# Expert weights streamed one matrix at a time: 1024 columns in 4 KB rows, eight column blocks open in three PSUM banks

## The chip, the cores and the metric

The kernel runs on one core of one Trainium2 chip. The metric is the device time of one execution in microseconds (us); lower is better. All times below come from the runs of the kernel before and from one execution of it under the profiler.

## What is computed

A hybrid encoder block (convolution branch, state-space branch, gated merge) is followed by a mixture of 16 experts. The change lies in the experts alone. Each expert picks the `cap` = 130 tokens of 1040 with the highest affinity, and 16 experts of 1024 x 2048 (gate and up) and 2048 x 1024 (down) run on them, all in float32:

```python
def expert_choice_ffn(xn, w_router, w_gate, w_up, w_down):
    b, T, d = xn.shape
    cap = CAPACITY_FACTOR * T // N_EXPERTS
    aff = jax.nn.softmax(jnp.einsum('btd,de->bte', xn, w_router).astype(jnp.float32), axis=-1)
    top_aff, top_idx = lax.top_k(jnp.swapaxes(aff, 1, 2), cap)
    xg = xn[bi, top_idx]
    hg = jnp.einsum('becd,edf->becf', xg, w_gate)
    hu = jnp.einsum('becd,edf->becf', xg, w_up)
    y = jnp.einsum('becf,efd->becd', jax.nn.silu(hg) * hu, w_down)
    y = y * top_aff[..., None].astype(y.dtype)
    return jnp.zeros_like(xn).at[bi, top_idx].add(y)
```

## The kernel before

The expert stage is a list of 64 steps, four to an expert (`steps`, the loop at the end of the listing), from about 1650 us to the end of the span. A step takes 512 columns of the gate matrix and the same 512 of the up matrix. `load_gu` brings them in four tiles of 1 MB (`wst`, two to a matrix, rows of 2 KB in HBM) into a ring of 11 buffers, which the down matrix shares (`bring`, two tiles to a step, rows of 4 KB); all of these loads go out on SP's queue. The loads run `RUN` = 2 steps ahead.

TensorE multiplies in float16, so a weight tile is split first into a high part `wh` and a rest `wl`. `norms` sums the squares of each tile on ScalarE (into `junk`, L1137); `scales` turns these into one power-of-two scale per matrix (a CAST to `sqb`, two small matmuls into a PSUM tile `rp`, L1109, and five tiny VectorE operations `sc`); `convert` then writes `wh` (half on ScalarE, L1148, half on VectorE, L1149) and `wl` (VectorE, L1151). All of this is done one step ahead. Expert 0's first two steps are native: its raw float32 tiles go into the matmuls.

In `gate_up`, `pair(p)` takes two column blocks of 128 of either matrix: 24 matmuls of 130 columns each fill one block (8 row blocks, times `wh`·x0, `wh`·x1, `wl`·x0), and two blocks share a PSUM tile `gu`, of which there are three. ScalarE then reads the gate tile (`sil`, L1180) and VectorE multiplies in the up tile (`ac`, L1181). A step has two such pairs of 96 matmuls each. From expert 1 on, 16 float32 matmuls of the expert before stand behind each pair (`down`, L1203, PSUM tiles `dn`).

Once per expert three other things pass through. `put` turns the finished outputs of the expert before (four transposes into `rp` for each of four pieces), scales them on VectorE (`yo0`, `yo1`, L1221) and adds them to HBM by indirect DMAs from POOL (L1222); `yo0` comes in step 0 of the next expert, `yo1` at that step's end. `route` (step 1) makes the list of the next expert's tokens (18 small matmuls into `rp`, L1061) and has POOL gather them (`xg`, two indirect DMAs, L1070). `turn` (end of step 2) transposes `xg` on TensorE in four quarters of 8 transposes (L1098), each into an `rp` tile that ScalarE copies to `xT` (L1100). There are two `rp` buffers, and `put`, `route`, `scales` and `turn` share them.

The order on each engine is set when the kernel is built, by a scheduler that keeps each engine's own order fixed at run time; `tc.high_priority` moves an operation forward in it. So an operation that waits holds up all that stands behind it on its engine.

## Time and profile before

| what | value |
|---|---|
| device time, median of 3 runs | 3004.99 us (2998.09 to 3011.6) |
| the profiled execution | 2988.87 us, span 2987.1 us |
| TensorE (PE) busy | 2750.6 us, 92% of the span |
| VectorE (DVE) / ScalarE (ACT) / GpSimd (POOL) busy | 75% / 57% / 21% |
| mean granted TensorE clock | 0.961 of full speed |
| twelve experts, 1828.8 to 2785.4 us | PE 933.46 us busy of 956.60, clock 0.99, DMA share 0.95 |

PE is the matmul engine, PEld its weight loads, SP the engine that issues the weight loads. "busy" counts the time in which at least one instruction of the engine is under way; matmuls overlap in the pipeline, so a matmul's own duration is longer than the distance to the next. A wait is idle time of an engine ended by what is named behind the arrow.

### The profile page before, as it was taken

To read this page: it belongs to the slowest core of one execution; us is meant where nothing else is said; L and a number is where in the kernel's file an instruction comes from. 1 tells how busy PE (TensorE), PEld (TensorE's weight loads), DVE (VectorE), ACT (ScalarE), POOL (GpSimd) and SP (SyncE) were. 2 spreads that over 40 slices of the span, in tenths; PEclk is the share of its full clock that TensorE was granted. 3 is DMA by queue.
4 is the path that set the end of the run, shared out by engine and by line. 5 is a ranking of instruction groups with operands and counts; after the bars stand their busy time and mean duration, and the time that the engine had idled before them with its cause. 6 is when DMAs were issued, how large, how long until landed. Compare 5 with 4: busy or idle time off the path is not lost. (4 is left out here: it accounts for less than half of the span.)

```text
span 2987.1 us, 65478 instructions
## 1 busy us (share of the span) xinstructions
PE 2750.6 (92%) x27584; PEld 2359.5 (79%) x27584; DVE 2240.1 (75%) x3023; ACT 1713.3 (57%) x2549; POOL 616.6 (21%) x688
## 2 busy tenths in 40 slices
PE   6989989989997998989998889999999999999995
PEld 4656656655665666989967889999999999999995
DVE  6867896998896799988456677777767676777663
ACT  6567656565665542444223656766666666666743
POOL 2131132132123113330000002222211112222213
PEclk8999989999998999999999899999999999999997
DMA  5356576565566554424345889999999999999994
GB/s 146 96 160 198 173 214 202 156 197 181 181 180 207 161 176 131 161 61 139 107 141 181 301 291 332 337 327 333 336 322 330 325 332 322 332 338 330 334 323 141
DMA packets 337783, 689.77 MB, mean 231 GB/s; under 512 B 38241, under 2 KB 98049, under 8 KB 337481
## 3 DMA queue, kind: packets, MB, share of 16 engines
q1 hardware_dynamic: 284784, 528.74, 51.4%
q0 software_dynamic: 42624, 125.45, 14.7%
q10 hardware_dynamic: 10080, 31.40, 3.3%
q8 instruction: 216, 3.54, 0.5%
q14 instruction: 79, 0.65, 0.1%
HBM read 610.48 MB, written 75.01 MB: 229 GB/s over the span
## 5 line engine op out<-in xcount | busy, mean ns | idle before, releaser
L97 PE MATMUL gu<-xT,wh 128*128 128x130 f16 x3968 | 698.1, 222 | 2.3 <-ACT sil L1180 2.3
L98 PE MATMUL gu<-xT,wh 128*128 128x130 f16 x3968 | 697.9, 220 | 0.0
L99 PE MATMUL gu<-xT,wl 128*128 128x130 f16 x3968 | 697.1, 220 | 0.8 <-DVE wl L1151 0.8
L1137 ACT ACTIVATE junk<-wst 128x2048 bf16<-128x2048 f32 x248 | 473.7, 1910 | 386.3 <-DMA wst<-in_w_exp_gate_dram 313.1
L1151 DVE SCALAR_TENSOR_TENSOR wl<-wst,sc,wh 128x2048 f16<-128x2048 f32 x248 | 572.7, 2346 | 24.3 <-ACT wh L1148 20.7
L98 PEld LDWEIGHTS <-wh 128*128 128x128 f16 x4856 | 480.4, 99 | 75.5 <-issue 32.6
L97 PEld LDWEIGHTS <-wh 128*128 128x128 f16 x4856 | 474.7, 98 | 52.1 <-issue 9.7
L99 PEld LDWEIGHTS <-wl 128*128 128x128 f16 x4832 | 470.0, 97 | 45.2 <-DVE wl L1151 1.1
L1203 PE MATMUL dn<-ac,wst 128*128 128x130 f32 x3840 | 459.3, 277 | 0.0
L1203 PEld LDWEIGHTS dn<-ac,wst 128*128 128x128 f32 x3840 | 440.7, 191 | 0.0
L1222 POOL DMA_INDIRECT h<-yo,idx x60 | 181.5, 3025 | 910.2 <-DVE yo L1221 758.5
L339 DVE SCALAR_TENSOR_TENSOR co<-ci,ct,co 128x1040 f32<-128x1040 f32 x240 | 323.8, 1349 | 5.5 <-ACT co L336 3.8
L97 PE MATMUL mm<-uh,wh 128*128 128x346 f16 (+3 forms) x888 | 279.4, 315 | 17.4 <-ACT xt L404 8.1
L97 PE MATMUL mm<-uh,wl 128*128 128x346 f16 (+1 forms) x864 | 271.7, 314 | 13.3 <-ACT xt L404 7.0
L98 PE MATMUL mm<-ul,wh 128*128 128x346 f16 (+3 forms) x888 | 279.0, 314 | 0.0
L99 PE MATMUL mm<-uh,wh 128*128 128x346 f16 (+3 forms) x888 | 278.1, 314 | 0.0
L98 PE MATMUL mm<-ul,wl 128*128 128x346 f16 (+1 forms) x864 | 271.2, 314 | 0.0
L99 PE MATMUL mm<-uh,wl 128*128 128x346 f16 (+1 forms) x864 | 271.0, 314 | 0.0
L611 ACT ACTIVATE row<-row,cst 128x128 f32<-128x128 f32 (+1 forms) x576 | 170.8, 378 | 143.4 <-DMA row<-cs_d 123.9
L1148 ACT ACTIVATE wh<-wst,sc 128x2048 f16<-128x2048 f32 x124 | 241.2, 1994 | 16.1 <-DVE sc L1114 15.4
L385 DVE SCALAR_TENSOR_TENSOR po<-pre,sp,po 128x1040 f32<-128x1040 f32 x144 | 185.7, 1296 | 2.4 <-ACT po L382 2.0
L97 PE MATMUL mm<-yh,wh 128*128 128x346 f32 (+1 forms) x480 | 156.9, 333 | 15.6 <-ACT yh L796 8.4
(431 smaller groups left out, 4839.9 us busy)
## 6 DMA issues: line engine op xcount, KB each, us to landing
wst<-in_w_exp_gate_dram SPq DMA_DIRECT2D x128, 1024.0 KB, 7.9
wst<-in_w_exp_up_dram SPq DMA_DIRECT2D x128, 1024.0 KB, 9.7
wst<-in_w_exp_down_dram SPq DMA_DIRECT2D x128, 1024.0 KB, 9.9
wr<-in_w_in_dram POOLq DMA_DIRECT2D x70, 512.0 KB, 6.4
row<-cs_d SPq DMA_DIRECT2D x64, 512.0 KB, 5.0
xk<-xk_d SPq DMA_DIRECT2D x92, 256.0 KB, 3.5
er<-ecs_d SPq DMA_DIRECT2D x120, 128.0 KB, 3.7
xk_d<-xt POOLq DMA_DIRECT2D x40, 256.0 KB, 4.2
```

Of the source, the lines that this page charges most:

```text
L97: pe.matmul(ps, wh(k), xh(k), start=(k == 0), stop=False)
L98: pe.matmul(ps, wh(k), xl(k), start=False, stop=False)
L99: pe.matmul(ps, wl(k), xh(k), start=False, stop=(k == K - 1))
L339: dve.scalar_tensor_tensor(co, ci[:, m:m + T], ct[:, m:m + 1], co, op0=OP.mult, op1=OP.add)
L385: dve.scalar_tensor_tensor(po, pre[:, m:m + T], sp[:, j, m:m + 1], po, op0=OP.mult, op1=OP.add)
L611: act.activation(out=E[:L, j, :L], in_=E[:L, j, :L], func=AF.Relu, scale=-1.0, bias=cs)
L1137: act.activation(out=junk, in_=t[m][b], func=AF.Square, accum_out=sq[:, b, m:m + 1])
L1148: act.activation(out=wh[m][0], in_=t[m][0], func=AF.Copy, scale=sc[:, 1, m:m + 1])
L1151: dve.scalar_tensor_tensor(wl[m][b], t[m][b], sc[:, 1, m:m + 1], wh[m][b], op0=OP.mult, op1=OP.subtract)
L1203: pe.matmul(last["dn"][b // 3][:, b % 3], t[:, k, b * P:b * P + P], ac[:, 2 * i + k], start=(i + k == 0 and b % 3 == 0), stop=(i == 7 and ...
L1222: nc.gpsimd.indirect_dma_start(out=h2_d[b], in_=yo[:, h], in_offset=None, compute_op=OP.add, out_offset=bass.IndirectOffsetOnAxis(ap=r.idx ...
```

## The change

A step still has four tiles of 1 MB, but all from one matrix: 1024 columns of gate in steps 0 and 2, the same columns of up in steps 1 and 3. Each tile holds 256 rows of 4 KB. A step has one scale where it had two. Its eight column blocks are open together, in three PSUM tiles of 3, 3 and 2 blocks, and the loop over rows is outermost: `rows_(b)` runs all 48 matmuls that need tile `b`, so all three `gu` tiles are in use from the first tile to the last, and are read only after it: by ScalarE in a gate step (silu straight into `ac`, the `sil` tile is gone), by VectorE in an up step (into `ac` in place). The matmuls, norms, `wh` and `wl` are as many and as large as before. `turn` becomes a generator: its first quarter comes at the end of step 1, the others at points inside step 2, and its copies to `xT` get a high priority.

```diff
-        junk = sel.tile([P, 4, 512], BF, name="junk")
+        junk = sel.tile([P, 2, D], BF, name="junk")
...
                 for i in range(2):
                     for k0 in (0, 4):
+                        yield
                         ps = mps2.tile([P, 4, 2, HC + 1], F16, name="rp")
...
+                        with tc.high_priority(offset=300):
+                            act.activation(out=self.xT[i][:, k0:k0 + 4].rearrange("p k (h c) -> p k h c", h=2),
+                                           in_=ps[:, :, :, :HC], func=AF.Copy)
...
-            for i in range(2):
-                pe.matmul(ps, onesb, sq[:, i], start=(i == 0), stop=(i == 1))
+            for i in range(4):
+                pe.matmul(ps, onesb, sq[:, i:i + 1], start=(i == 0), stop=(i == 3))
...
-            for w in (w_exp_gate, w_exp_up):
-                for b in range(2):
-                    t = ring.tile([P, 4, 512], F32, name="wst")
...
-                    nc.sync.dma_start(t, w[0, e, 512 * b:512 * b + 512, 512 * q:512 * q + 512].rearrange(
+            for b in range(4):
+                t = ring.tile([P, 2, D], F32, name="wst")
...
+                w = w_exp_up if q % 2 else w_exp_gate
+                nc.sync.dma_start(t, w[0, e, 256 * b:256 * b + 256, q // 2 * D:q // 2 * D + D].rearrange(
...
+            for b in range(4):
+                wh.append(split.tile([P, 2, D], F16, name="wh"))
+                wl.append(split.tile([P, 2, D], F16, name="wl", bufs=6))
+                if b % 2:
+                    dve.tensor_scalar_mul(wh[b], t[b], sc[:, 1:2])
+                else:
+                    act.activation(out=wh[b], in_=t[b], func=AF.Copy, scale=sc[:, 1:2])
+                dve.scalar_tensor_tensor(wl[b], t[b], sc[:, 1:2], wh[b], op0=OP.mult, op1=OP.subtract)
...
+            def rows_(b):
+                if b == 0:
+                    sums.extend(mps2.tile([P, 3, CAP], F32, name="gu", bufs=3) for _ in range(3))
+                for k in (2 * b, 2 * b + 1):
+                    for f in range(KD):
+                        ps, cols = sums[f // 3][:, f % 3], slice(f * P, f * P + P)
+                        opens, ends = k == 0 and f % 3 == 0, k == KD - 1
...
+                        pe.matmul(ps, wh[b][:, k % 2, cols], xT[0][:, k], start=opens, stop=False, skip_group_check=True)
+                        pe.matmul(ps, wh[b][:, k % 2, cols], xT[1][:, k], start=False, stop=False, skip_group_check=True)
+                        pe.matmul(ps, wl[b][:, k % 2, cols], xT[0][:, k], start=False, stop=ends, skip_group_check=True)
+                if b < 3:
+                    return
...
+                        if q % 2:
+                            dve.scalar_tensor_tensor(a_, sums[i][:, :n], s, a_, op0=OP.mult, op1=OP.mult)
                         else:
+                            act.activation(out=a_, in_=sums[i][:, :n], func=AF.Silu, scale=s)
...
-            pair(0)
+            part(0)
+            next(turning, None)
+            part(1)
             next(done, None)
             if prev:
                 down(2 * q, ds[0], prev[0])
+            next(turning, None)
             if raw:
                 ready[coming] = convert(raw, sq)
-            pair(1)
+            part(2)
+            next(turning, None)
+            part(3)
             next(done, None)
             if prev:
                 down(2 * q + 1, ds[1], prev[0])
-            if e + 1 < NE and q == 2:
-                nxt.turn()
+            if e + 1 < NE and q == 1:
+                turning = nxt.turn()
+                next(turning)
+            elif q == 2:
+                for _ in turning:
+                    pass
```

Three places where the built order moves, all in expert 8 (expert 9 is being routed); the other experts from 3 to 13 read alike. In the rows `_123` numbers a buffer, and x3 is a row that stands three times.

TensorE at the first quarter of the turn. `rp` is written by the transposes of `xg`, `dn` by the down matmuls, `gu` by the gate and up matmuls. Before, at the end of step 2:

```order
L1203 MATMUL dn_25908<-ac_24551,wst_26393 128x130 x2
L1098 LDWEIGHTS xg_26108
L1098 MATMUL rp_26671<-identh_115,xg_26108 128x65
...
L1098 MATMUL rp_26681<-identh_115,xg_26110 128x65
L97 LDWEIGHTS wh_26536
L97 MATMUL gu_26728<-xT0_25448,wh_26536 128x130
...
L98 MATMUL gu_26728<-xT1_25449,wh_26536 128x130
L1098 LDWEIGHTS xg_26108
L1098 MATMUL rp_26691<-identh_115,xg_26108 128x65
```

With the change, at the end of step 1:

```order
L1211 MATMUL dn_25840<-ac_24493,wst_26047 128x130 x2
L1099 LDWEIGHTS xg_26040
L1099 MATMUL rp_26391<-identh_115,xg_26040 128x65
...
L1099 MATMUL rp_26391<-identh_115,xg_26042 128x65
L1211 MATMUL dn_25838<-ac_24493,wst_26323 128x130 x3
L1211 MATMUL dn_25839<-ac_24493,wst_26323 128x130 x2
L1176 LDWEIGHTS wh_26190
L1176 MATMUL gu_26340<-xT0_25108,wh_26190 128x130
```

Before, two quarters stand together and the other two follow 29 `gu` matmuls later, in the first 1.7 us of step 3. With the change one quarter stands at the end of step 1, the second follows after 96 `gu` and 11 `dn` matmuls, the third after 48 more `gu`, and the fourth after 48 `gu` and 16 `dn`. The 18 matmuls of `route` move inside step 1 from behind the third `gu` matmul to behind the 61st.

VectorE from step 0 to step 1. `wl` and `wh` are the next step's weights, `yo1` the second half of the outputs of expert 7, `idx` the tokens of expert 9. Before:

```order
L1151 SCALAR_TENSOR_TENSOR wl_25940<-wst_25494,sc_25930,wh_25936 128x2048
L1149 TENSOR_SCALAR wh_25939<-wst_25500,sc_25930 128x2048
L1181 SCALAR_TENSOR_TENSOR ac_25772<-gu_26001,sc_25629,sil_26050 128x260
L1221 TENSOR_SCALAR yo1_26053<-rp_26054,wgt_22443 65x512
L1221 TENSOR_SCALAR yo1_26053<-rp_26061,wgt_22443 65x512
L1151 SCALAR_TENSOR_TENSOR wl_25943<-wst_25500,sc_25930,wh_25939 128x2048
L1151 SCALAR_TENSOR_TENSOR wl_25942<-wst_25498,sc_25930,wh_25938 128x2048
L1112 TENSOR_SCALAR sc_26252<-rp_26249 128x2
L1066 TENSOR_REDUCE idx_26105<-rp_26086 65x2
L1074 TENSOR_REDUCE wgt_26106<-rp_26086 65x2
L1054 TENSOR_TENSOR oh_27305<-iot_116,slot_111 128x1170
```

With the change:

```order
L1108 CAST sqb_26177<-sq_26057 128x4
L1153 SCALAR_TENSOR_TENSOR wl_25871<-wst_25430,sc_25864,wh_25870 128x2048
L1153 SCALAR_TENSOR_TENSOR wl_25875<-wst_25432,sc_25864,wh_25874 128x2048
L1153 SCALAR_TENSOR_TENSOR wl_25879<-wst_25434,sc_25864,wh_25878 128x2048
L1153 SCALAR_TENSOR_TENSOR wl_25883<-wst_25436,sc_25864,wh_25882 128x2048
L1229 TENSOR_SCALAR yo1_25985<-rp_25986,wgt_22399 65x512
L1229 TENSOR_SCALAR yo1_25985<-rp_25993,wgt_22399 65x512
L1114 TENSOR_SCALAR sc_26184<-rp_26179 128x1
L1066 TENSOR_REDUCE idx_26037<-rp_26018 65x2
L1115 TENSOR_SCALAR sc_26184<-sc_26184 128x1
L1074 TENSOR_REDUCE wgt_26038<-rp_26018 65x2
L1054 TENSOR_TENSOR oh_27229<-iot_116,slot_111 128x1170
```

Two of the four `wl` stood behind `yo1`; now all four stand ahead of it, and behind it come `oh` and small operations. In the same way the three reads of an up step's `gu` tiles come behind the four `wl` of the next step.

POOL over two experts: `h2_0` and `h2_1` are the adds of `yo0` and `yo1`, `xg` the gathers. Before:

```order
L1070 DMA xg_24887<-hn_d_81,idx_24884 65x2048
L1070 DMA xg_24889<-hn_d_81,idx_24884 65x2048
L1222 DMA h2_0_82<-yo0_25891,idx_22442 1040x512 x2
L1222 DMA h2_1_83<-yo1_26053,idx_22442 1040x512 x2
L1070 DMA xg_26108<-hn_d_81,idx_26105 65x2048
L1070 DMA xg_26110<-hn_d_81,idx_26105 65x2048
```

With the change:

```order
L1230 DMA h2_0_82<-yo0_25823,idx_22398 1040x512 x2
L1230 DMA h2_1_83<-yo1_25985,idx_22398 1040x512
L1070 DMA xg_26040<-hn_d_81,idx_26037 65x2048
L1070 DMA xg_26042<-hn_d_81,idx_26037 65x2048
L1230 DMA h2_1_83<-yo1_25985,idx_22398 1040x512
```

The gathers stood behind both adds of `yo1`; now they stand between the two.

## Rows read from the trace of the kernel before

**Rows 1.** The page, part 1: busy time of each engine, share of span.

```profile
PE 2750.6 (92%) x27584; PEld 2359.5 (79%) x27584; DVE 2240.1 (75%) x3023; ACT 1713.3 (57%) x2549; POOL 616.6 (21%) x688
```

**Rows 2.** Busy time by stretch; last three columns: granted clock, DMA share, GB/s.

```profile
1720.00:1800.00 80.00, 70.17 (x1066) 69.35 (x1064) 64.75 (x103) 48.95 (x49) 4.09 (x2) 0.94 0.85 302
1828.80:2785.40 956.60, 933.46 (x13179) 926.38 (x13177) 680.63 (x757) 632.68 (x660) 209.71 (x73) 0.99 0.95 331
```

**Rows 3.** Waits, 1750 to 2900 us: total, times, longest.

```profile
ACT junk L1137 <- DMA wst<-in_w_exp_gate_dram: 296.6, 76, 6.7
...
PE rp L1098 <- ACT xT L1100: 19.3, 13, 2.7
...
PE rp L1098 <- DMA xg<-hn_d,idx: 8.7, 2, 6.0
...
PE rp L1109 <- DVE sqb L1106: 3.8, 5, 1.6
```

**Rows 4.** Timeline of PE at expert 8's turn: start, us, instruction [idle before].

```profile
2342.32 0.65 PE L1098 MATMUL rp<-identh,xg 65*128 65x65 f16 x16
...
2344.18 0.22 PE L97 MATMUL gu<-xT,wh 128*128 128x130 f16 x1
...
2344.41 0.22 PE L98 MATMUL gu<-xT,wh 128*128 128x130 f16 x1
2346.72 0.90 PE L1098 MATMUL rp<-identh,xg 65*128 65x65 f16 x16 [2.10 <-ACT xT L1100]
```

**Rows 5.** Timeline of ACT at the same turn.

```profile
2338.27 0.46 ACT L1180 ACTIVATE sil<-gu,sc 128x260 f32<-128x260 f32 x1
2344.18 1.91 ACT L1137 ACTIVATE junk<-wst 128x2048 bf16<-128x2048 f32 x1 [5.45 <-DMA wst<-in_w_exp_gate_dram]
2345.99 0.19 ACT L1137 ACTIVATION_READ_ACCUMULATOR junk<-wst 128x1 f32 x1
2346.09 1.08 ACT L1100 ACTIVATE xT<-rp 128x520 f16<-128x520 f16 x2
```

**Rows 6.** Groups by line and form, 1750 to 2900 us: count, busy, mean ns.

```profile
L1151 DVE SCALAR_TENSOR_TENSOR wl<-wst,sc,wh 128x2048 f16<-128x2048 f32 x232 | 536.1, 2346 | 24.3 <-ACT wh L1148 20.7 <-DVE wh L1149 0.5 <-DMA wst<-in_w_exp_up_dram 0.2
L1203 PE MATMUL dn<-ac,wst 128*128 128x130 f32 x3643 | 435.6, 277 | 0.0
...
L1181 DVE SCALAR_TENSOR_TENSOR ac<-gu,sc,sil 128x260 f32<-128x260 f32 x116 | 56.1, 484 | 92.1 <-PE gu L99 81.7 <-ACT sil L1180 10.4
L1180 ACT ACTIVATE sil<-gu,sc 128x260 f32<-128x260 f32 x116 | 54.0, 466 | 14.9 <-PE gu L99 14.9
...
L1210 ACT ACTIVATE yT<-dn 128x390 f32<-128x390 f32 x28 | 12.0, 481 | 0.0
L1109 PE MATMUL rp<-sqb,onesb 128*128 128x2 bf16 x116 | 11.8, 164 | 4.0 <-DVE sqb L1106 3.8
...
L1210 ACT ACTIVATE yT<-dn 128x260 f32<-128x260 f32 x14 | 5.4, 387 | 0.0
```

**Rows 7.** Timeline of PE where expert 8's step 1 begins.

```profile
2304.74 0.22 PE L97 MATMUL gu<-xT,wh 128*128 128x130 f16 x1
...
2305.31 0.19 PE L1109 MATMUL rp<-sqb,onesb 128*128 128x2 bf16 x2
```

**Rows 8.** Timeline of DVE there.

```profile
2303.16 1.40 DVE L1221 TENSOR_SCALAR yo<-rp,wgt 65x512 f32<-65x512 f32 x2
2304.48 4.60 DVE L1151 SCALAR_TENSOR_TENSOR wl<-wst,sc,wh 128x2048 f16<-128x2048 f32 x2
2309.00 0.15 DVE L1112 TENSOR_SCALAR sc<-rp 128x2 f32<-128x2 f32 x1
```

**Rows 9.** Timeline of POOL in expert 8.

```profile
2291.94 1.48 POOL L1222 DMA_INDIRECT h<-yo,idx  x1 [46.65 <-DVE yo L1221]
2296.75 1.58 POOL L1222 DMA_INDIRECT h<-yo,idx  x1 [3.34 <-DMA h<-yo,idx]
2304.19 6.21 POOL L1222 DMA_INDIRECT h<-yo,idx  x1 [5.87 <-DVE yo L1221]
2317.96 1.51 POOL L1222 DMA_INDIRECT h<-yo,idx  x1 [7.56 <-DVE wl L1151]
2319.78 2.87 POOL L1070 DMA_INDIRECT xg<-hn_d,idx  x1 [0.30 <-DVE sqb L1106]
2322.95 1.94 POOL L1070 DMA_INDIRECT xg<-hn_d,idx  x1 [0.30 <-issue]
```

**Rows 10.** DMA issues, 1828.8 to 2785.4 us: count, median us to landing.

```profile
xg<-hn_d,idx POOLq DMA_INDIRECT x24, 9.8
```

**Rows 11.** DMA, 1660 to 1720 us in 40 slices, issues below.

```profile
GB/s 365 27 0 0 0 81 362 406 390 386 389 395 242 234 188 107 147 407 322 388 391 395 391 389 375 388 385 399 370 385 386 389 393 408 411 393 395 391 102 33
...
wst<-in_w_exp_up_dram SPq DMA_DIRECT2D x7, 1024.0 KB, 9.7
wst<-in_w_exp_gate_dram SPq DMA_DIRECT2D x7, 1024.0 KB, 9.3
```

More of the change, by code (lines that the diff above doesn't have):

```diff
@@ L1144, in convert @@
                 sc = scales(sq, sx[:, 0:1])
-            wh = [[split.tile([P, 4, 512], F16, name="wh") for _ in range(2)] for _ in range(2)]
-            wl = [[split.tile([P, 4, 512], F16, name="wl", bufs=6) for _ in range(2)] for _ in range(2)]
-            for m in range(2):
-                act.activation(out=wh[m][0], in_=t[m][0], func=AF.Copy, scale=sc[:, 1, m:m + 1])
-                dve.tensor_scalar_mul(wh[m][1], t[m][1], sc[:, 1, m:m + 1])
-                for b in (1, 0):
-                    dve.scalar_tensor_tensor(wl[m][b], t[m][b], sc[:, 1, m:m + 1], wh[m][b], op0=OP.mult,
-                                             op1=OP.subtract)
+            wh, wl = [], []
+            for b in range(4):
+                wh.append(split.tile([P, 2, D], F16, name="wh"))
[5 more added lines that the diff above has]
+                dve.scalar_tensor_tensor(wl[b], t[b], sc[:, 1:2], wh[b], op0=OP.mult, op1=OP.subtract)
             return wh, wl, sc
@@ L1160, in gate_up @@
                 wh, wl, sc = t
-            def pair(p):
-                pss = []
-                for m in range(2):
-                    ps = mps2.tile([P, 2, CAP], F32, name="gu", bufs=3)
-                    for f in range(2):
-                        cols = slice((2 * p + f) * P, (2 * p + f) * P + P)
-                        if native:
-                            for k in range(KD):
-                                pe.matmul(ps[:, f], t[m][k // 4][:, k % 4, cols], first.xf[:, k], start=(k == 0),
-                                          stop=(k == KD - 1))
-                        else:
-                            mm3(ps[:, f], lambda k: wh[m][k // 4][:, k % 4, cols], lambda k: wl[m][k // 4][:, k % 4, cols],
-                                lambda k: xT[0][:, k], lambda k: xT[1][:, k], KD)
-                    pss.append(ps)
-                s0, s1 = (sx[:, 0:1], sx[:, 0:1]) if native else (sc[:, 2, 0:1], sc[:, 2, 1:2])
-                b0 = 4 * q + 2 * p
-                with tc.high_priority(offset=300):
-                    sil = mo.tile([P, 2, CAP], F32, name="sil")
-                    act.activation(out=sil, in_=pss[0], func=AF.Silu, scale=s0)
-                    dve.scalar_tensor_tensor(ac[:, b0:b0 + 2], pss[1], s1, sil, op0=OP.mult, op1=OP.mult)
@@ L1183, in gate_up @@
-            return pair
+            sums = []
+            def rows_(b):
[5 more added lines that the diff above has]
+                        opens, ends = k == 0 and f % 3 == 0, k == KD - 1
+                        if native:
+                            pe.matmul(ps, t[b][:, k % 2, cols], first.xf[:, k], start=opens, stop=ends,
+                                      skip_group_check=True)
+                            continue
+                        pe.matmul(ps, wh[b][:, k % 2, cols], xT[0][:, k], start=opens, stop=False, skip_group_check=True)
[3 more added lines that the diff above has]
+                    return
+                s = sx[:, 0:1] if native else sc[:, 2:3]
+                with tc.high_priority(offset=300):
+                    for i in range(3):
+                        n = min(3, KD - 3 * i)
+                        a_ = ac[:, KD * (q // 2) + 3 * i:KD * (q // 2) + 3 * i + n]
+                        if q % 2:
+                            dve.scalar_tensor_tensor(a_, sums[i][:, :n], s, a_, op0=OP.mult, op1=OP.mult)
+                        else:
+                            act.activation(out=a_, in_=sums[i][:, :n], func=AF.Silu, scale=s)
@@ L1185, in bring @@
+            return rows_
         def bring(e, i):
@@ L1272, in tile_block @@
             cur.whole()
-            cur.turn()
+            for _ in cur.turn():
+                pass
         done = iter(())
+        turning = iter(())
         steps = [(e, q) for e in range(NE) for q in range(4)]
@@ L1300, in tile_block @@
                 sq = norms(raw)
-            pair = gate_up(ready.pop((e, q)) if (e, q) in ready else tiles.pop((e, q)), q, cur.xT, ac,
+            part = gate_up(ready.pop((e, q)) if (e, q) in ready else tiles.pop((e, q)), q, cur.xT, ac,
                            None if e else cur)
-            pair(0)
+            part(0)
+            next(turning, None)
+            part(1)
             next(done, None)
@@ L1312, in tile_block @@
                 down(2 * q + 1, ds[1], prev[0])
-            if e + 1 < NE and q == 2:
-                nxt.turn()
+            if e + 1 < NE and q == 1:
[3 more added lines that the diff above has]
+                for _ in turning:
+                    pass
             if q == 3:
```

35 lines of the change are left out of this document (15 added, 20 removed).

## The prediction

> **What bounds the kernel now.** I read the page's first part, then the stretches, the waits, and the timeline at one turn. The page has TensorE busy for 92% of the span and VectorE, the next of the engines, for 75% [rows 1]. In the stretch that the change touches it is closer still: over twelve experts TensorE is busy 933.46 of 956.60 us, with the clock at 0.99 and the DMA engines at 0.95 [rows 2]. What is left to win there is 23.1 us of idle, 1.93 us an expert, and little more. An expert takes 956.6 / 12 = 79.7 us.
>
> The waits say whose idle it is. From 1750 to 2900 us TensorE waited 13 times, 19.3 us in all, at the turn for ScalarE's copy to `xT`, five times for the scale's CAST (3.8 us), and once, in two pieces, for expert 2's tokens (8.7 us) [rows 3]. ScalarE's 296.6 us of waiting for gate tiles is by far the longest row there, but it is a wait of an engine with room; it costs something only where TensorE waits for ScalarE. The turn is that place. Two quarters fill both `rp` buffers, 29 `gu` matmuls later the third needs one back, and TensorE stops at 2344.41 until 2346.72 [rows 4]. ScalarE has nothing to do from 2338.7 on, yet the copy comes after a norm that waits until 2344.18 for a gate tile [rows 5]. The order, not the work, makes the stall.
>
> **The change, part by part.** The sum is against the profiled execution, 2988.87 us (its span plus 1.8 us); that is 16.1 us below the median of the runs, 3004.99, and I add the difference to the median. 14 turns lie in the stretch.
>
> *Turn.* From the last `gu` before the wait to the first transpose behind it are 2.31 us [rows 4]; `gu` matmuls otherwise start 0.0575 us apart (four of them from 2344.18 to 2344.41), so a wait costs 2.31 - 0.06 - 2.10 = 0.15 us more than its idle shows. 13 such waits cost 19.3 + 13 x 0.15 = 21.3 us. After the change the second quarter follows the first by 96 `gu` (96 x 0.0575 = 5.5 us) and 11 `dn` matmuls. 16 of these take 32 records, so 435.6 / 3643 x 32 = 3.83 us [rows 6], 11 take 2.6. ScalarE thus has 8.1 us for a 0.6 us copy, and each quarter finds a free `rp`. A norm in front that waits for its tile can take 6.7 us at the worst [rows 3] plus 2.1 of its own, which just reaches that. I take the whole -21.3; the other end is half, -10. The 16 transposes of the second half also took 0.90 us against 0.65 for the first 16 [rows 4], once more for a buffer: 14 x 0.25 = -3.5.
>
> *Scale.* The CAST's waits are 3.8 + 5 x 0.15 = 4.6 us; the scale keeps its place between `dn` matmuls, so they may stay or go: 0 to -4.6, I take -2. Four one-column matmuls replace two: a pair takes 0.19 us [rows 7] where one takes 0.164 [rows 6], so 0.026 us each, and 62 steps x 2 x 0.026 = +3.2 us.
>
> *Banks.* This is the new wait. All three `gu` tiles are full when a step ends, and the next step cannot begin before the first is read. The cover is the 16 `dn` matmuls between the steps, 3.83 us. A read of 390 columns takes on ScalarE 0.09 us more than one of 260 (0.481 against 0.387) [rows 6], so the reads are about 0.56, 0.56 and 0.47 us on ScalarE and 0.58, 0.58 and 0.48 on VectorE, from 0.466 and 0.484 [rows 6]. If the engine is free, the cover hides them six times over. VectorE in an up step reads behind the `wl` of the next step. One `wl` in the way (2.35 us) still fits: 2.35 + 0.58 = 2.93. Two do not: 4.69 + 0.58 = 5.27, which is 1.44 us too late. There are 28 up steps. Bounds 0 and 28 x 1.44 = 40 us; since VectorE is 71% busy (680.63 of 956.60 [rows 2]), nearer to the free case, 0.15 us each, +4.2.
>
> *Expert 0* has no `dn` between its steps. Its two gate steps are read by ScalarE, which may be held by one norm each, 1.91 + 0.19 us [rows 5]: +4.2. Bounds 0 and twice the longest wait for a tile, 2 x 6.7 = 13.4 [rows 3]. The 8.7 us for expert 2's tokens stay: POOL is late there in both orders.
>
> *`yo1` behind four `wl`.* Now `route`'s matmuls, 61 x 0.0575 = 3.5 us into step 1, need the `rp` buffers that `yo1` empties last. In the trace the same pieces, `yo1` and the `wl` together, end at 2309.0 [rows 8], 4.3 us after step 1 began [rows 7]. TensorE may wait 0.8 us: 0 to 14 x 0.8 = 11, and as VectorE has lost a few small operations I take 0.2 each, +3.
>
> *The gather, earlier.* The first quarter now stands at the end of step 1. Steps 1 and 2 take 2342.32 - 2304.74 = 37.6 us [rows 4, 7]; with route in the first of them, step 1 is some 19.3 us. POOL's chain in the new order: the first `yo1` add begins at about 3.6 us into step 1; it takes 1.5 us (1.48, 1.58, 1.51 [rows 9]); the token list comes at about 5.6; the two gathers start 0.3 + 2.87 us apart [rows 9], the second at 5.9 + 3.2 = 9.1, and land 9.8 us later [rows 10]: 18.9. That is in time by 0.4 us, a thin margin. Bounds 0 and the case below; I take +2.
>
> *4 KB rows.* In expert 0, where only tiles in 2 KB rows are loaded, the slices run at 385 to 411 GB/s [rows 11]; the long stretch has 331 [rows 2]. So 2 KB rows are not what holds the DMA engines there; free buffers are. The first cost is that ScalarE's tiles come late, and TensorE's share of this is already in the terms above. What else TensorE idles is 14 x 1.93 - 19.3 - 3.8 = 3.9 us: bounds 0 and -3.9, I take -2. The Trainium skill ("Perfetto Trace Analysis", DMA Optimizations) says that going from 2 KB to 4 KB transfers can improve throughput dramatically when a kernel is held by its DMAs. By it this term would be the full -3.9; the slices of expert 0 do not bear it out.
>
> Sum: -21.3 - 3.5 - 2 + 3.2 + 4.2 + 4.2 + 3 + 2 - 2 = **-12.2 us**, 2976.7 for a profiled execution and 2992.8 against the median.
>
> **The rivals.** *Everything comes free.* No new wait appears and tiles come sooner: -21.3 - 3.5 - 4.6 + 3.2 - 3.9 = -30.1, 2975. For it speaks that every new wait has a cover several times its size; against, that expert 0 has none.
>
> *The banks take it back.* VectorE comes with two `wl` in hand in half of the up steps: 28 x 0.5 x 1.44 = 20 in place of 4.2, -12.2 + 16 = +4, 3009: no change. For it speaks the order, which puts the reads behind four `wl`; against it, 29% of VectorE's time is idle. The Trainium skill ("Perfetto Trace Analysis", Optimizing Tensor Performance, Matmuls) wants independent groups to rotate through the banks, so that reading one overlaps the next group's matmuls, which speaks against holding three banks for a whole step. The trace before shows that rotation with `sil` and `ac` hidden, and no row shows what its loss costs.
>
> *Slower: the first quarter waits for the gather.* The add of `yo1` took 6.21 us, not 1.5, where two `wl` ran directly behind `yo1` (2304.19, beside 2304.48 to 2309.08) [rows 8, 9]. If it still does, or the list comes late by as much, the gather lands at 18.9 + 4.7 = 23.6, 4.3 us behind the quarter; 14 x 4.3 = 60 in place of the 2 above gives +46, 3051. It decides from the point where the waits outweigh the gain: 12.2 / 14, some 0.9 us an expert, so a gather that lands 20.2 us or later into step 1. A delay of 2 us gives 28 - 2 - 12.2 = +14, 3019. Against it: behind `yo1` now come `oh` and small operations, and a gap until the scale's matmuls are done, and one add instead of two stands in front.
>
> **How the numbers follow.** A measurement of this kernel can tell about 0.5%, 15 us. My forecast, a part of the turn's waits won and a part given back, gets 0.51 and covers -25 to 0; its middle lies just inside the 15 us, so 0.20 of it is faster and 0.31 the same. All free: 0.23, faster. The banks take it back: 0.09, the same. The gather: 0.17, mostly slower by 14 us or more. Together faster 0.43, same 0.40, slower 0.17. The range goes from 2970 (all free, with a little of hidden slack) to 3022 (a gather 2.2 us late); beyond it lie most of the slower case's upper half and a few in a hundred below.
>
> **What would show it.** Right: no wait of the turn's transposes for `xT` left, an expert at about 78.5 us (79.7 less the terms that repeat, 16.4 / 14), PE idle near 1 us an expert. Banks: waits of the first `gu` of a step for VectorE's `ac`, or ScalarE's silu in expert 0, named at each boundary. Gather: a wait of the first quarter for the `xg` DMA, 14 times, and an add of `yo1` above 3 us on POOL. `yo1`: route's first matmul waiting for it. DMA: the share falls below 0.95 at the same bytes if 4 KB rows are cheaper; that alone moves nothing. I am wrong if TensorE's stretch stays at 79.7 us with the turn's waits gone and no new wait named, for then the idle was never what held it; or if the gather row stands at the top.

## The result, and the profile after

The changed kernel is slower: 3044.91 us (median of four runs, 3041.68 to 3050.02) beside 3001.59 us for the kernel before in the same comparison; the ratio is 1.0143 [1.0126, 1.0160], about +43 us. The profiled execution took 3046.21 us, with a span of 3044.5 us.

The page's first part and the windows, to be laid beside [rows 1, 2] (the second window is again twelve experts, from one `put` to the one twelve experts later; the columns are the busy times of PE, PEld, DVE, ACT and POOL, then granted clock, DMA share and GB/s):

```profile
PE 2768.7 (91%) x27708; PEld 2375.0 (78%) x27708; DVE 2232.4 (73%) x2991; ACT 1713.1 (56%) x2517; POOL 525.5 (17%) x688
...
1720.00:1800.00 80.00, 72.25 (x1117) 71.06 (x1114) 63.09 (x124) 47.40 (x45) 4.39 (x2) 0.94 0.78 279
1909.70:2906.90 997.20, 944.21 (x13276) 936.57 (x13274) 672.39 (x733) 633.27 (x635) 126.77 (x72) 0.98 0.90 317
```

Twelve experts take 997.20 us in place of 956.60, 83.1 us each in place of 79.7: +40.6 of the +57.4 by which the two spans differ. TensorE's idle time there grew from 23.1 to 997.20 - 944.21 = 53.0 us, +29.9, and its busy time by 944.21 - 933.46 = 10.8. The other 17 us lie ahead of that stretch, in the experts 0 and 1. The DMA share fell from 0.95 to 0.90, the same bytes over a longer time: the loads have become less pressed, not more.

The waits from 1750 to 2950 us, to be laid beside [rows 3]:

```profile
ACT junk L1138 <- DMA wst<-in_w_exp_gate_dram: 203.0, 85, 9.3
ACT junk L1138 <- DMA wst<-in_w_exp_up_dram: 180.7, 72, 6.2
DVE wl L1153 <- ACT wh L1152: 115.8, 43, 4.2
PE gu L1176 <- DVE ac L1187: 56.3, 23, 4.8
...
PE rp L1099 <- DMA xg<-hn_d,idx: 4.4, 3, 2.0
PE gu L1176 <- ACT wh L1152: 3.9, 1, 3.9
PE rp L1061 <- DVE yo L1229: 0.5, 1, 0.5
```

The turn's waits for `xT` are gone, as forecast. In their place stands one row: the first `gu` matmul of a step waits for VectorE's read (`ac`) of the tiles of the step before, 23 times, 2.4 us on the mean: 13 times at the end of a step 3, ten times at the end of a step 1. VectorE itself waits 115.8 us for ScalarE's `wh` (20.7 before), and ScalarE 383.7 us for tiles (296.6 for gate and 53.5 for up tiles before, 350.1 together).

One such wait, at the end of expert 8's step 3 (an up step), on three engines. ScalarE:

```profile
2303.29 1.91 ACT L1138 ACTIVATE junk<-wst 128x2048 bf16<-128x2048 f32 x1 [2.00 <-DMA wst<-in_w_exp_up_dram]
...
2305.20 3.88 ACT L1152 ACTIVATE wh<-wst,sc 128x2048 f16<-128x2048 f32 x2
```

VectorE:

```profile
2300.85 0.15 DVE L1116 TENSOR_SCALAR sc<-sc 128x1 int32<-128x1 int32 x1
...
2303.44 0.21 DVE L1118 TENSOR_SCALAR sc<-sc,sx 128x1 f32<-128x1 f32 x1
2307.22 9.14 DVE L1153 SCALAR_TENSOR_TENSOR wl<-wst,sc,wh 128x2048 f16<-128x2048 f32 x4 [3.58 <-ACT wh L1152]
...
2316.35 1.55 DVE L1187 SCALAR_TENSOR_TENSOR ac<-gu,sc,ac 128x390 f32<-128x390 f32 x3
```

TensorE:

```profile
2309.96 3.79 PE L1211 MATMUL dn<-ac,wst 128*128 128x130 f32 x32
2317.02 0.27 PE L1176 MATMUL gu<-xT,wh 128*128 128x130 f16 x1 [3.27 <-DVE ac L1187]
2317.08 0.32 PE L1177 MATMUL gu<-xT,wh 128*128 128x130 f16 x1
2317.19 0.32 PE L1178 MATMUL gu<-xT,wl 128*128 128x130 f16 x1
```

Read from the bottom up. TensorE has no more `dn` matmuls from 2313.75 on and waits 3.27 us for a read of 0.62 us. The read stands behind four `wl` of 9.14 us together. These could have begun at 2303.65, but the first needs `wh`, and VectorE waits 3.58 us for it: more than TensorE's whole wait. `wh` could have begun at 2301.29: the scale that it needs was there (L1116, done at 2301.00), and ScalarE had ended the norm before. But in ScalarE's order one more norm stands ahead, of a tile that only the step after next needs, and that norm waits until 2303.29 for its load; `wh` begins at 2305.20. So a wait for a tile that nobody needs yet goes through ScalarE and VectorE to TensorE.

The loads may close a loop, since SP waits for the buffers that `wl` sets free. From 1900 to 2800 us:

```profile
SPq L1129 <- DVE wl L1153: 371.3, 129, 9.1
```

A late `wl` makes a late load, and that a late norm. How much the loop adds to itself was not taken apart. SP's wait alone does not show it: it is 335.6 us in the version below whose norms stand behind `wh`, where TensorE does not wait for the reads.

TensorE pays once more after about half of these waits, in its clock. Windows of 4 us around the same place, and the last one behind a shorter wait, of 1.21 us, that ends at 2277.45:

```profile
2312.00:2316.00 4.00, 1.75 (x16) 1.58 (x15) 4.00 (x2) 1.40 (x3) 0.00 (x0) 1.00 0.89 338
2316.00:2320.00 4.00, 2.98 (x28) 2.98 (x28) 1.89 (x5) 2.19 (x3) 0.00 (x0) 0.63 1.02 412
2320.00:2324.00 4.00, 4.00 (x69) 4.00 (x68) 0.00 (x0) 3.44 (x5) 0.00 (x0) 0.95 1.03 416
...
2277.45:2281.45 4.00, 4.00 (x71) 4.00 (x71) 0.88 (x2) 2.10 (x3) 0.00 (x0) 1.00 1.02 413
```

The granted clock is 0.63 in the window behind the wait and 0.95 in the next. The `gu` matmuls behind the wait start 0.11 us apart (2317.08, 2317.19), the lower level of 1.2 GHz, where 0.0575 us is the distance at 2.4 GHz. In the 4 us behind twelve of the 13 waits at the end of a step 3 (2.35 to 4.84 us long) the clock reads 0.50 to 0.66; behind the thirteenth (2.13 us) and the ten of step 1 (0.21 to 1.73 us) it reads 1.00. What this costs shows beside a version of the same steps and matmuls in which TensorE never waits (norms behind `wh`, old turn, among the experiments below), again over twelve experts:

```profile
1903.37:2823.46 920.09, 920.09 (x13275) 916.76 (x13274) 672.48 (x734) 637.73 (x636) 152.99 (x73) 1.00 0.95 344
```

Against it the change spends 997.20 - 920.09 = 77.1 us more: 53.0 of idle and 944.21 - 920.09 = 24.1 of longer busy time. By an estimate (4 us times what the clock lacks to 1.00, over the eleven of these windows that lie in the stretch) 18 of the 24 are the clock's. Beside the kernel before the busy time grew by only 10.8, because that had lost busy time to its own waits as well (11.5 us, below).

### The profile page after: what moved, and what is told of

It is laid out like the page before. It is cut to its first block, busy times and chain, and to the rows that moved or that the text cites. A ratio compares the mean times of both kernels' runs of the same rounds, so it can differ in the third digit from the quotient of the medians.

```text
span 3044.5 us, 65416 instructions
## 1 busy us (share of the span) xinstructions
PE 2768.7 (91%) x27708; PEld 2375.0 (78%) x27708; DVE 2232.4 (73%) x2991; ACT 1713.1 (56%) x2517; POOL 525.5 (17%) x688
## 5 line engine op out<-in xcount | busy, mean ns | idle before, releaser
L1176 PE MATMUL gu<-xT,wh 128*128 128x130 f16 x3968 | 704.3, 224 | 61.4 <-DVE ac L1187 56.3
L1177 PEld LDWEIGHTS <-wh 128*128 128x128 f16 x3968 | 396.0, 100 | 63.1 <-issue 62.0
L1176 PEld LDWEIGHTS <-wh 128*128 128x128 f16 x3968 | 395.1, 100 | 3.9 <-ACT wh L1152 3.9
L1178 PEld LDWEIGHTS <-wl 128*128 128x128 f16 x3968 | 395.1, 100 | 0.3 <-DVE wl L1153 0.3
L1230 POOL DMA_INDIRECT h<-yo,idx x60 | 95.9, 1598 | 1036.5 <-DVE yo L1229 961.9
```

What stands on the lines that cost most here:

```text
L1176: pe.matmul(ps, wh[b][:, k % 2, cols], xT[0][:, k], start=opens, stop=False, skip_group_check=True)
L1177: pe.matmul(ps, wh[b][:, k % 2, cols], xT[1][:, k], start=False, stop=False, skip_group_check=True)
L1178: pe.matmul(ps, wl[b][:, k % 2, cols], xT[0][:, k], start=False, stop=ends, skip_group_check=True)
```

## The experiments

What stands ahead of each `wh` on ScalarE was in the built order, before any run. This is the changed kernel's, from the silu reads at the end of expert 8's step 2 on (`wh` at the second row is the one at 2305.20 above; x2 means two in a row):

```
L1138 ACTIVATE junk,sq<-wst 128x2048 x2
L1152 ACTIVATE wh<-wst,sc 128x2048 x2
L1138 ACTIVATE junk,sq<-wst 128x2048 x2
L1218 ACTIVATE yT<-dn 128x390
L1138 ACTIVATE junk,sq<-wst 128x2048
L1218 ACTIVATE yT<-dn 128x390
L1218 ACTIVATE yT<-dn 128x260
L1138 ACTIVATE junk,sq<-wst 128x2048 x3
L1152 ACTIVATE wh<-wst,sc 128x2048 x2
L1189 ACTIVATE ac<-gu,sc 128x390 x2
L1189 ACTIVATE ac<-gu,sc 128x260
L1138 ACTIVATE junk,sq<-wst 128x2048 x3
L1152 ACTIVATE wh<-wst,sc 128x2048 x2
```

Each pair of `wh` needs the four norms of its own step; norms beyond these belong to the step after. Counted so, 2 norms too many stand ahead of the first pair here, 2 + 6 - 4 = 4 ahead of the second, and 4 + 3 - 4 = 3 ahead of the third. Over an expert's four steps the changed kernel has 3, 4, 2, 4 (13), the kernel before 3, 1, 3, 4 (11). I call them the norms ahead.

Two theories stood against each other. By the first, VectorE's *work* ahead of the reads (four `wl`) holds TensorE; by the second it is VectorE's *waiting*, which comes from the norms ahead. Beside them the row size and the new turn had to be cleared. In the expectations A is the order (reads behind four `wl` that wait for `wh`), B the row size, C the held banks; L, from the fifth experiment on, is the loop of norm, `wl`, buffer and load. The kernel before is measured anew in each of three sets of runs: 2992.92 us for the first four, 2993.3 for the next four and 2990.74 for the last four; every ratio is against it.

**Reads behind two `wl` in place of four.** The splits of tiles 2 and 3 move behind the reads of an up step (`piece(bs)` splits the tiles in `bs`):

```diff
+            piece(range(2 if late else 4))
+            if late:
+                late.append(lambda: piece((2, 3)))
...
+            if raw and late:
+                with tc.issue_after(last["read"].ins):
+                    late[1]()
```

> The changed kernel, but in an up step the second half of the next step's weights (wh and wl of tiles 2 and 3) is put behind VectorE's three reads of the gu tiles, so that two wl instead of four stand ahead of a read. Theory A (order): the 56.3 us that TensorE waits for VectorE's ac, in 23 waits, come from the reads standing behind four wl, which wait for ScalarE's wh, which stands behind a norm that waits for a tile. Then these waits fall below 15 us and the time to 2995 to 3012 us. Theory B (rows): tiles in 4 KB rows land later and the waits are theirs: no gain, 3035 to 3055 us. Theory C (banks): three banks held to the end of a step leave no cover in any order: over half of the waits stay, 3020 to 3045 us.

3054.23 us, ratio 1.0207 [1.0172, 1.0242]. The waits, 1750 to 2950 us:

```profile
DVE wl L1155 <- ACT wh L1154: 179.9, 54, 6.1
PE rp L1061 <- DVE yo L1236: 46.8, 13, 3.8
...
PE gu L1182 <- DVE ac L1193: 4.2, 6, 1.3
```

The reads are nearly free (4.2 us in place of 56.3), as theory A expected, but its time (2995 to 3012) did not come: nothing is won. TensorE now waits 46.8 us for `yo1`, which stands behind the four `wl` of step 1's weights, as it does in the change, where this wait was 0.5. VectorE waits more for `wh` than in the change (179.9 in place of 115.8), and its CAST of the scale 80.8 us for the norms (13.1 in the change). Where the `wl` stand only chooses who meets the late engine.

**Norms behind both `wh`.** The norms ahead become 0, in the changed kernel; all else stays in the program text, though the scheduler then also shifts some `dn` and scale matmuls.

```diff
-            for b in range(4):
-                act.activation(out=junk, in_=t[b], func=AF.Square, accum_out=sq[:, b:b + 1])
+            with tc.issue_after(last["wh"].ins) if "wh" in last else nullcontext():
+                for b in range(4):
+                    act.activation(out=junk, in_=t[b], func=AF.Square, accum_out=sq[:, b:b + 1])
...
-                    act.activation(out=wh[b], in_=t[b], func=AF.Copy, scale=sc[:, 1:2])
+                    last["wh"] = act.activation(out=wh[b], in_=t[b], func=AF.Copy, scale=sc[:, 1:2])
```

> The changed kernel, but on ScalarE the norms of the step after next stand behind both wh of the next step, so that no wh waits behind a norm that waits for a tile. The reads stay behind four wl. Theory A: VectorE's 116 us of waiting for wh fall below 40, the reads come 2 to 3.5 us sooner, TensorE's waits for ac fall from 56 to below 25 us, and the time to 3005 to 3025 us; a part can come back because the scale now follows later norms. Theory B: 3035 to 3055 us. Theory C: 3030 to 3050 us.

2955.71 us, ratio 0.9893 [0.9855, 0.9932]: 89 us faster than the changed kernel by the medians, 75 by the ratios (0.9893 and 1.0143), faster than the kernel before, and far below what any of the three theories gave. Below I call this version the mended change. Windows:

```profile
1900.00:2800.00 900.00, 892.51 (x12862) 887.73 (x12862) 648.77 (x707) 610.18 (x617) 137.42 (x70) 1.00 0.95 340
```

TensorE idles 7.5 us in 900, all of it for `xg`. The reads still stand behind four `wl` (VectorE, the same kind of place):

```profile
2260.58 9.13 DVE L1154 SCALAR_TENSOR_TENSOR wl<-wst,sc,wh 128x2048 f16<-128x2048 f32 x4
2269.63 1.54 DVE L1188 SCALAR_TENSOR_TENSOR ac<-gu,sc,ac 128x390 f32<-128x390 f32 x3
```

Here the read still comes late, 4.56 us behind the start of the `dn` at 2265.07, but the scheduler had put more `dn` matmuls ahead of the next `gu`, so this place alone is no clean test. The version with one norm ahead, below, is: four `wl`, the same 32 `dn` rows as in the change, and no wait. So the waiting decides, not the work.

**The changed kernel with rows of 2 KB.** Each tile comes in two loads of 512 columns:

```diff
-                nc.sync.dma_start(t, w[0, e, 256 * b:256 * b + 256, q // 2 * D:q // 2 * D + D].rearrange(
...
+                for c in (0, 512):
+                    nc.sync.dma_start(t[:, :, c:c + 512], w[0, e, 256 * b:256 * b + 256, q // 2 * D + c:q // 2 * D + c + 512]
...
```

> The changed kernel with the same tiles and the same order, but each gate and up tile comes as two DMAs of 2 KB rows instead of one of 4 KB rows, so twice as many packets. Theory A: the row size is not what matters; 3035 to 3065 us, with TensorE's waits for ac between 45 and 75 us. Theory B: the rows of before bring the gain back: below 3020 us. Theory C: as A, 3035 to 3065 us.

3044.86 us, ratio 1.0182 [1.0138, 1.0226], beside 3044.91 us and a ratio of 1.0143 [1.0126, 1.0160] for the change as it is; the wait for `ac` is 58.8 us in 23 times. The intervals overlap, and the row size has no part in the loss that these runs can tell.

**The spread turn alone, in the kernel before.** Two quarters at the end of step 1 and two in step 2, with the copies' high priority:

```diff
-            if e + 1 < NE and q == 2:
-                nxt.turn()
+            if e + 1 < NE and q == 1:
+                turning = nxt.turn()
+                next(turning)
+                next(turning)
+            elif q == 2:
+                for _ in turning:
+                    pass
```

> The kernel before, with nothing of the change but the turn: its quarters spread (the first at the end of step 1, the others inside step 2), and the copies to xT at a high priority. Steps, tiles, rows and banks are those of before. Theory A: the 19.3 us of waits for xT go and nothing takes their place: 0.4 to 0.9% faster than before, 2975 to 2990 us. A rival says that the waits only move to the scale's matmuls or to xg, which share the rp tiles: within 0.3% of before.

3095.11 us, ratio 1.0357 [1.0323, 1.0392], far above both expectations. TensorE, 1750 to 2950 us:

```profile
PE rp L1099 <- DMA xg<-hn_d,idx: 114.0, 28, 7.6
```

POOL, one expert:

```profile
2090.27 6.20 POOL L1224 DMA_INDIRECT h<-yo,idx  x1 [3.47 <-DVE yo L1223]
2104.24 2.18 POOL L1224 DMA_INDIRECT h<-yo,idx  x1 [7.77 <-DVE ac L1183]
2106.73 1.69 POOL L1070 DMA_INDIRECT xg<-hn_d,idx  x1 [0.30 <-issue]
```

Here POOL keeps the order of before, with both adds ahead of the gathers, and the first add takes 6.20 us. This is the prediction's slower rival, in a kernel whose order makes it true; in the changed kernel POOL's order puts the gathers ahead of the second add, and it does not happen. The test is not of the turn alone: two quarters, not one, stand at the end of step 1, and the norms ahead have become 3, 4, 2, 4 here as well.

**The kernel before with its norms behind `wh`.** The same edit as in the second experiment, on the kernel before; the new steps, the 4 KB rows and the new turn are all absent.

> The kernel before, with nothing of the change, but with the same order on ScalarE as in the run with wh first: the norms of the step after next stand behind both wh of the next step. Theory L (loop): a norm that waits for a tile holds up wh, so wl ends later, so the buffers that wl frees are refilled later, so the tiles two steps on land later; before, TensorE has room enough to bear most of it, and loses 1.93 us an expert. Then ScalarE's 297 us of waiting for gate tiles nearly vanish, the turn's copies come at once, and the time is 0.5 to 1.2% below before (2955 to 2980 us). Rival P (the change's steps are what gains): the order is worth nothing in the old steps, within 0.4% of before.

2949.47 us, ratio 0.9850 [0.9817, 0.9884]. This is the fastest of all versions, a little below the forecast range, and beats both kernels; against the mended change it is 6 us less, with intervals that overlap. Windows, over twelve experts:

```profile
1888.30:2810.30 922.00, 922.00 (x13180) 918.49 (x13178) 681.85 (x757) 642.61 (x660) 213.96 (x72) 1.00 0.98 343
```

TensorE is busy in all of it, 76.8 us an expert. Against the 956.60 us before [rows 2] that is 34.6 us less: the 23.1 of idle, and 933.46 - 922.00 = 11.5 of busy time, with the clock at 1.00 in place of 0.99. The norms' waits for tiles, 296.6 us before [rows 3], are 0.9 us from 1900 to 2800 us:

```profile
ACT junk L1138 <- DMA wst<-in_w_exp_up_dram: 0.9, 3, 0.3
```

**Norms behind `wh`, and one other part of the change undone.** With 2 KB rows:

> The run with wh first, with each gate and up tile loaded as two DMAs of 2 KB rows. Theory L: with the loop open the loads have slack and the row size matters no more than it did in the changed kernel: within 0.4% of wh first, 2945 to 2968 us. Rival B: once the order is mended the 4 KB rows are what gains: above 2970 us.

2956.76 us, ratio 0.9885 [0.9854, 0.9916]. With the turn as before, also without its copies' high priority:

```diff
-            if e + 1 < NE and q == 1:
-                turning = nxt.turn()
-                next(turning)
-            elif q == 2:
-                for _ in turning:
-                    pass
+            if e + 1 < NE and q == 2:
+                nxt.turn()
```

> The run with wh first, with the turn as before: one piece at the end of step 2, copies to xT at no special priority. Theory L: without a norm that waits in front of the copies the old turn costs little: 2950 to 2968 us, with less than 6 us of waits for xT. Rival: the spread turn is itself worth the 19 to 25 us that the prediction gave it: 2970 to 2982 us.

2956.07 us, ratio 0.9874 [0.9843, 0.9906]. Neither differs from the 2955.71 of the mended change beyond the intervals, some 0.3% to either side. Once the norms are in place, neither the 4 KB rows nor the spread turn are worth anything that these runs can tell:

```profile
1900.00:2800.00 900.00, 900.00 (x12984) 896.70 (x12982) 658.80 (x718) 623.83 (x622) 152.99 (x72) 1.00 0.96 344
```

That row is of the kernel with the old turn; its quarters stand as they did before the change, and TensorE never stops for them. The turn's stall of before came from the norm in front of the copy, too.

**One, two, three norms ahead.** The changed kernel, with the edit of the second experiment only for tiles from 1, 2 or 3 on:

```diff
+                with tc.issue_after(last["wh"].ins) if "wh" in last and b >= 3 else nullcontext():
+                    act.activation(out=junk, in_=t[b], func=AF.Square, accum_out=sq[:, b:b + 1])
```

> The run with wh first, but the first of the four norms may again stand ahead of the two wh (in the changed kernel two to four stand there). Theory L says that it is a matter of how late the last norm ahead of wh gets its tile: between wh first and the changed kernel, nearer to wh first, 2955 to 2990 us, with ScalarE's waits for tiles back in part (50 to 200 us). Theory C (banks) has nothing to say about it. If the first tile of a step always lands early, no difference from wh first.

> The run with wh first, but two of the four norms of the step after next may stand ahead of the two wh, in every step. With none or one ahead there was no loss; in the changed kernel 3, 4, 2 and 4 stand there in the four steps of an expert. Theory L: the loop closes when the last norm ahead of wh gets its tile later than the scale is ready; so between the one-norm run and the changed kernel, 2952 to 3000 us, with TensorE's waits for ac below 20 us. Theory C (banks): no relation to this number.

> As the run before it, with three norms allowed ahead of wh (3, 3, 2 and 3 stand there; the changed kernel has 3, 4, 2 and 4). Theory L: slower than with two, 2975 to 3035 us, and the waits of wl for wh and of TensorE for ac are back in part. If the time is that of wh first, only the fourth norm counts.

| version | norms ahead per expert | median, us | ratio | TensorE for `ac` / VectorE for `wh`, us |
|---|---|---|---|---|
| norms behind `wh` | 0 | 2955.71 | 0.9893 [0.9855, 0.9932] | none / none |
| one ahead | 4 | 2954.45 | 0.9879 [0.9848, 0.9910] | none / none |
| two | 8 | 2958.89 | 0.9905 [0.9882, 0.9928] | 6.5 / 29.1 |
| three | 11 | 2987.47 | 0.9993 [0.9978, 1.0008] | 22.7 / 78.3 |
| the change | 13 | 3044.91 | 1.0143 [1.0126, 1.0160] | 56.3 / 115.8 |

With one norm ahead ScalarE's waits for tiles are back (134.9 us in 27 times for gate tiles), and cost nothing. An up step's end in this kernel shows why, VectorE ahead of TensorE:

```profile
2257.08 9.13 DVE L1154 SCALAR_TENSOR_TENSOR wl<-wst,sc,wh 128x2048 f16<-128x2048 f32 x4
2266.13 1.14 DVE L1188 SCALAR_TENSOR_TENSOR ac<-gu,sc,ac 128x390 f32<-128x390 f32 x2
```

```profile
2264.19 3.79 PE L1212 MATMUL dn<-ac,wst 128*128 128x130 f32 x32
2267.82 0.22 PE L1177 MATMUL gu<-xT,wh 128*128 128x130 f16 x1
```

The first read begins 1.94 us behind the step's last `gu` matmul, well inside the 3.79 us of `dn`; in the changed kernel it was 2316.35 - 2309.96 = 6.39. The cost is not in proportion to the count: nothing for four, about 30 us for eleven, 75 (by the ratios) to 89 (by the medians) for thirteen. The last step of the ladder, from three norms to the change, is not clean, since with these edits the scheduler also puts the scale's matmuls of every fourth step later.

**The change with the old turn.** Here the turn alone is undone, by the same edit as just before the ladder, and the norms are left to the scheduler. The scheduler then gives 3, 1, 3, 4 norms ahead, as in the kernel before.

> The changed kernel with its steps, tiles and banks, but the turn of before. The scheduler then puts 3, 1, 3 and 4 norms ahead of wh, as in the kernel before, where the changed kernel has 3, 4, 2 and 4. Theory L: the smaller number in one step opens the loop in part, so the time falls although the turn's waits come back: 2990 to 3035 us. The prediction's own sum (the turn alone worth 25 us): slower than the changed kernel, 3050 to 3075 us.

3021.19 us, ratio 1.0101 [1.0079, 1.0123]: 24 us faster than the change by the medians, 13 by the ratios, though the turn's waits are back:

```profile
DVE wl L1151 <- ACT wh L1150: 99.4, 34, 5.2
...
PE rp L1098 <- ACT xT L1100: 21.7, 10, 3.7
PE rp L1109 <- DVE sqb L1106: 16.2, 11, 2.4
```

So the spread turn, with what the scheduler moved for it, cost more than the 21.7 us of waits that it saved. That the norms' places are the cause fits the counts (11 in place of 13) but was not shown by itself; and the count alone does not fix the time, since the three-norm version, with the spread turn and eleven ahead (3, 3, 2, 3), took 2987.47 us.

**A late spread turn in the kernel before.** Its quarters run from the start of step 2 to the end of step 3, so that the gather is in time; the norms ahead become 2, 4, 4, 3.

> The kernel before with nothing but a spread turn, this time late: the quarters stand behind the first and second half of steps 2 and 3, where xg has long landed, and POOL gathers between the two adds of yo1. 2, 4, 4 and 3 norms stand ahead of wh (before 3, 1, 3 and 4). If the turn's waits are all there is: 0.5 to 0.9% below before, 2968 to 2985 us. Theory L: the waits for xT go, but the norms' places cost as much or more: within 0.4% of before or up to 1% slower, 2982 to 3025 us.

2987.64 us, ratio 0.9991 [0.9975, 1.0007]. No wait for `xT` is left to speak of (0.3 us). In its place:

```profile
PE rp L1221 <- ACT yT L1212: 14.6, 12, 2.1
PE gu L99 <- DVE wl L1153: 9.4, 13, 1.0
```

Together 24.0 us, where the turn had cost 19.3. The stall went to the next operations that stand behind a norm, as at the `yT` for which TensorE then waits 2.09 us:

```profile
2045.75 1.91 ACT L1139 ACTIVATE junk<-wst 128x2048 bf16<-128x2048 f32 x1 [3.38 <-DMA wst<-in_w_exp_gate_dram]
...
2047.66 0.75 ACT L1212 ACTIVATE yT<-dn 128x390 f32<-128x390 f32 x2
```

Laid side by side, the versions show that the norms ahead do more harm in the new steps than in the old. With none ahead the ratio is 0.9850 in the old steps and 0.9893 in the new ones; with 11 ahead and the old turn it is 1 (the kernel before) and 1.0101; with 13 ahead and a spread turn 0.9991 (this version) and 1.0143 (the change).

## Why the prediction was wrong

The forecast was 2992.8 us, in a range of 2970 to 3022; measured were 3044.91.

*What bounds the kernel.* The prediction saw ScalarE's 296.6 us of waits for tiles, and set them aside: "it is a wait of an engine with room; it costs something only where TensorE waits for ScalarE. The turn is that place." This is the step that failed; in the sum it is the term *Banks* that carries it. ScalarE's order also puts norms ahead of `wh`, VectorE's `wl` wait for `wh`, and the reads wait for `wl`. Removing those waits gave 1.5% in the kernel before and 2.5 to 2.9% in the changed one (by the ratios, 0.9893 / 1.0143 = 0.975; by the medians, 2955.71 / 3044.91 = 0.971). The turn was one place of several. Nor was "23.1 us of idle, 1.93 us an expert, and little more" all that could be won: the kernel before lost 34.6 us in those twelve experts, 11.5 of them in busy time.

*Banks.* +4.2 us, bounds 0 and 40; measured are 56.3 us of waits, beside their clock, so the term alone takes the forecast to a loss. The mechanism was named, a wait of the first `gu` for `ac` behind `wl`. Two things were mis-sized. "since VectorE is 71% busy (680.63 of 956.60 [rows 2]), nearer to the free case" priced an engine with a fixed order by its mean share: the 29% are no reserve, they are time in which it waits. And the upper bound counted only VectorE's work in the way (two `wl` in hand); with the 3.58 us for `wh` added, a single wait came to as much as 4.8 us against the 1.44 of the bound. The rival "the banks take it back" had the mechanism and the direction, priced at 20 us.

The Trainium skill ("Perfetto Trace Analysis", Optimizing Tensor Performance, Matmuls), which asks that groups rotate through the banks so that a read overlaps the next matmuls, was weighed there. The trace of the change agrees as far as TensorE waits 23 times for such a read; the versions with the norms mended do not need it: with all three tiles held for a whole step, and the old turn, TensorE is busy 900.00 of 900.00 us. Held banks take away slack, and what used it up was the order on ScalarE: without norms ahead the new steps cost nothing that these runs can tell.

*Clock.* The sum put 0.15 us on each wait, from one of the turn's waits. Behind twelve of the new ones the clock reads 0.50 to 0.66 for 4 us, and an estimated 18 us of TensorE's busy time come from it in twelve experts. No term stood for that.

*Turn.* The 13 waits for `xT` went, as forecast (-21.3 and a part of -3.5). The old turn costs nothing once the norms are mended, and in the changed kernel the new one loses, as far as the counts tell, by moving norms. The prediction read the order at the turn right ("the order, not the work, makes the stall") and did not ask the same of the other places.

*Gather.* In time: `xg` cost 4.4 us from 1750 to 2950 us, three waits, where [rows 3] had 8.7. The add of `yo1` behind which the gathers stand took 1.44 us:

```profile
2341.16 1.44 POOL L1230 DMA_INDIRECT h<-yo,idx  x1 [8.87 <-DVE yo L1229]
2343.77 2.62 POOL L1070 DMA_INDIRECT xg<-hn_d,idx  x1 [1.17 <-DVE sc L1115]
```

That the add is long where `wl` run directly behind `yo1` (6.21 us in [rows 9], 6.20 with the spread turn alone) and short here was the prediction's argument against the slower rival, and held. The Trainium skill ("SBUF — State Buffer", SBUF: two separate sides) has a rule for it: VectorE and GpSimd share a pair of ports that one of them holds for a whole instruction while the other is blocked; VectorE takes it with an operation in a two-port mode or, against a GpSimd operation that reads SBUF, with two inputs in SBUF, as `wl` has. The two lengths agree with it; no run here separates it from other causes.

*Smaller terms.* `yo1` behind four `wl`: +3 forecast, 0.5 measured. Expert 0's banks: +4.2 forecast, 4.4 and 1.1 measured (two waits for silu reads, 1640 to 1830 us; the first is of a native step):

```profile
PE gu L1173 <- ACT ac L1189: 4.4, 1, 4.4
...
PE gu L1176 <- ACT ac L1189: 1.1, 1, 1.1
```

4 KB rows: -2 forecast; the medians are 0.05 us apart in one pair of versions and 1.05 in the other, so none that these runs can tell. The DMA engines do have less to do: with the norms behind `wh` and the same 340 GB/s (1900 to 2800 us) their share is 0.95 with 4 KB rows and 0.97 with 2 KB, and, as the prediction said, that alone moves nothing. Its reading of [rows 11] was not clean: the stretch also has two loads of 4 KB rows, and the slices of 408 and 411 GB/s are theirs for the most part.

```profile
wst<-in_w_exp_down_dram SPq DMA_DIRECT2D x2, 1024.0 KB, 12.7
```

Ahead of them, from 1691 to 1706 us, packets of 2 KB alone run at 387 GB/s, so its conclusion stands. The reads of 390 columns were forecast at 0.56 on ScalarE and 0.58 on VectorE and took 0.585 and 0.617. Of the other 11 of the 17 us by which experts 0 and 1 became longer, an estimated 8 are the same loss: TensorE waits 4.33 us for `ac` at the end of expert 1's step 3 (1901.42), and the clock reads 0.57 from 1900 to 1908 us (0.43 x 8 = 3.4). The rest was not followed up.

## What to carry to other kernels

A wait on an engine with room is free only if nothing behind it in that engine's fixed order is needed soon: follow the order from the wait to the next operation that another engine waits for, and on, to the engine that bounds the kernel. Work that is done ahead of its need (norms for the step after next) belongs behind the work of the next step, above all if it waits for loads; here that one line of order was worth more than new tiles, rows and turn together. When a change moves one operation, count again in the built order what stands ahead of every operation with a due time: the scheduler moves the others as well.

## What the runs showed of the hardware that was not expected

Behind a wait of 3.27 us the granted clock read 0.57 over the next 4 us (2317.02 to 2321.02), with matmuls 0.11 us apart, though the clock over twelve experts still read 0.98; in the versions without waits it read 1.00. So a mean clock of 0.99 (before) or 0.98 (the change) stood beside 11.5 and 24.1 us of longer busy time in twelve experts, which idle time does not show. And loads at 0.96 to 0.98 of the DMA engines' time, with 343 to 344 GB/s, did not hold TensorE at all (900.00 and 922.00 us busy without a gap), where the changed kernel had 0.90 and 317 GB/s: less load on the DMA engines went with the slower kernel.
